# Writing a gate vector to DRAM: one transfer of single values, or a transpose and 16 rows

## Chip, core and metric

The kernel runs on one core of a Trainium2 chip. The metric is the device time of one execution in microseconds; the median over several runs is compared. The core has TensorE (PE; PEld is its weight load), VectorE (DVE), ScalarE (ACT) and GpSimd (POOL), and SyncE (SP), which here issues nearly all DMA transfers. Each engine works through its own queue in order. A DMA queue entry waits on SP until what it needs is there, and whatever stands behind it waits too.

## What is computed

A two-layer decoder trunk on x of 256 tokens by 2048. Each layer has two sub-layers, a token mixer and a SwiGLU, four sub-layers in all (0 to 3), and each is

```
mod = silu(c) @ w + b
shift, scale, gate = split(mod, 3)
x <- LayerNorm(ALPHA * x + (1 + gate) * f(x * (1 + scale) + shift))
```

c is one vector of 2048, so shift, scale and gate are vectors of 2048 per sub-layer. f is in layer 0 an mLSTM and an RWKV-7 head group between an input and an output projection, in layer 1 a retention and a gated DeltaNet group, and in both layers a SwiGLU. All is in float32.

## The kernel before

The time goes into the products with the weights. The weights come from DRAM in tiles of 128 x 2048 float32 (1 MB), by `raw` (L667), into three buffers named raw. `split` (L689 on ScalarE, L690 on VectorE) cuts each into two parts hi and lo of type float32r, and `part` (L704, L705, L706) makes three products of them. A raw buffer is free again when its second part is split, and the next load is issued on SP.

The modulation is not a TensorE product. `ada` runs 192 units, 48 for each sub-layer; a unit loads a tile of 128 x 2048 through the same three raw buffers (some of the first ones through other buffers) and multiplies it on VectorE with silu(c) and sums along the row (L634), which gives one column of 128 values. `fill` strews these units between the units of the products at a given rate, up to a limit (`ada_limit`) for each stage. So the gate of a sub-layer is long complete, in most cases, before it is used. Units 32 to 47 of a sub-layer give the gate. At unit 47, L653 forms 1 + gate in the tile g1 (128 partitions x 16 columns: value 128 k + p of the gate stands in partition p, column k).

The residual needs the gate along the free dimension, the same in all 128 partitions. For that g1 goes to a scratch tile in DRAM, gate_row, of 16 rows of 128 values (L655), and `gate_rows` fetches the 8 KB row into all 128 partitions, 1 MB in SBUF (L661). `gate_rows` is called in `mix_out` (sub-layers 0 and 2, with a buffer of the pool a) and in `ffn` ahead of the second third's down products (sub-layers 1 and 3, with a buffer of the pool y). The users of the gate are `residual` (L833) and `last_sum` (L845) on VectorE.

Small buffers go round by tag. t2 has three buffers, used for the rows of the layer norm (`ln_rows`, L819), blocks of x (`x_block`, L802), the tables of the retention heads (L1656), the weights of the mLSTM heads and others. The PSUM tag c has two banks, used for instance by the convolution's transposes (L1318). Tiles of one tag are opened in program order.

The order of the instructions on each engine is not that of the program. Class `Plan` takes all instructions with their dependences, simulates the engines with a cost for each kind of instruction, puts at each moment the ready instruction with the lowest program number next (weight loads and splits are moved up by 2000), and imposes the order that comes out. It gives a transfer the time of its bytes and a fixed part. So any new instruction can shift the order of others, and one with a low number is taken as soon as its inputs and its buffer are there.

Of the kernel before, what the change touches and what calls it, by code (L numbers as in the profile page):

```python
# [12 lines left out]
F32 = mybir.dt.float32  # L13
F32R = mybir.dt.float32r
I32 = mybir.dt.int32
AF = mybir.ActivationFunctionType
# [5 lines left out]
P = 128  # L22
T = 256
NT = T // P
D = 2048
KT = D // P
# [499 lines left out]
class Trunk:  # L526
# [97 lines left out]
    def ada_unit(self, u, deep):  # L624
        nc, v = self.nc, self.nc.vector
        sub, i = divmod(u, 48)
        src = self.ins["ada"][u]
        if deep and i % 2:
            w = self.a8([P, D])
            nc.sync.dma_start(w[:], src)  # L630
        else:
            w = self.raw(src)
        m = self.mod
        v.scalar_tensor_tensor(w[:], w[:], 1.0, self.sc[:], ALU.mult, ALU.mult, accum_out=m[:, i:i + 1])  # L634
        ob = COLS["adab"][0] + 48 * sub
        if i < 32:
            if i % 8 < 7:
                return
            g = i // 8
            s = slice(4 * g, 4 * g + 4)  # L640
            sh, sc, bi = self.tiny([P, 4])[:], self.ab[:, sub, s], self.ab[:, sub, 16 + 4 * g:20 + 4 * g]
            v.tensor_tensor(sh, m[:, i - 7:i - 3], self.cols[:, ob + i - 7:ob + i - 3], ALU.add)
            v.scalar_tensor_tensor(sc, m[:, i - 3:i + 1], 1.0, self.cols[:, ob + i - 3:ob + i + 1], ALU.add, ALU.add)
            if sub == 0:
                v.tensor_copy(bi, sh)
            else:
                og, ol = COLS["lng"][0] + 16 * (sub - 1) + 4 * g, COLS["lnb"][0] + 16 * (sub - 1) + 4 * g
                v.tensor_tensor(bi, self.cols[:, ol:ol + 4], sc, ALU.mult)
                v.tensor_tensor(bi, bi, sh, ALU.add)
                v.tensor_tensor(sc, self.cols[:, og:og + 4], sc, ALU.mult)  # L650
            return
        if i == 47:
            v.scalar_tensor_tensor(self.g1[:], m[:, 32:48], 1.0, self.cols[:, ob + 32:ob + 48], ALU.add, ALU.add)  # L653
            self.gate_row = self.dram.tile([KT, P], F32, name=self.name("gate_row"))
            nc.sync.dma_start(self.gate_row[:].rearrange("k p -> p k"), self.g1[:])  # L655

    def gate_rows(self, room, sub):

        self.ada(max(0, 48 * sub + 48 - self.ada_next))
        gate = room([P, D])  # L660
        self.nc.sync.dma_start(gate[:], self.gate_row[:].rearrange("k p -> (k p)").unsqueeze(0).to_broadcast([P, D]))  # L661
        return gate


# [1140 lines left out]
```

## Time and profile before

| | |
|---|---|
| median of 3 runs | 2866.54 us (2863.94 to 2867.68) |
| the profiled execution | 2870.13 us, span 2868.4 us |
| mean granted TensorE clock | 0.970 |
| TensorE busy | 2701.2 us, 94% |
| VectorE, ScalarE, GpSimd busy | 71%, 44%, 2% |
| DMA | 683.80 MB in 118664 packets |
| weight loads of 1 MB, issue to landing | 4.7 to 5.5 us (median by source) |

How to read it: the span is from the first to the last instruction of the profiled execution. Busy time of an engine says little about what a stage waits for; views by stretches of time give the busy time of each engine in each, the clock that TensorE was granted (1.00 is full speed) and what the DMA engines moved. The wait views name for each waiting instruction what came last. Lines such as L655 are lines of the kernel before; `SPq` marks entries of SP's DMA queue.

### The profile page before, as it was taken

Reading aid. Unit: us, or ns where it says so; the run is one execution under the profiler, and the core shown is the slowest. Engines: PE = TensorE matmul, PEld = TensorE weight load, DVE = VectorE, ACT = ScalarE, POOL = GpSimd, SP = SyncE. Lnnn points to the kernel's source line nnn. Section 1 sums busy time; section 2 is a strip of 40 time slices with the busy share of each in tenths; the row PEclk is TensorE's granted clock in tenths of the full one; section 3 lists DMA queues with packets and bytes.
Section 4 is the critical chain, followed back from the end, with each engine's and each line's share of the span. In section 5 each row is a group of like instructions: output and inputs, shape, how many; then the busy total and the mean of one; then the engine's idle time right before and its main releaser. Section 6 shows DMA issues by size and latency. Waiting matters only on the chain.

```text
span 2868.4 us, 33238 instructions
## 1 busy us (share of the span) xinstructions
PE 2701.2 (94%) x12618; PEld 2215.9 (77%) x12618; DVE 2024.6 (71%) x3189; ACT 1261.6 (44%) x1668; POOL 69.3 (2%) x88
## 2 busy tenths in 40 slices
PE   3699998899999899999999899999989999999997
PEld 2577776787778788788787788788878888888886
DVE  7789578577867547768777798876786646557557
ACT  1365344437544344343445555344454444443442
POOL 0000000100000000000000010101000000000000
PEclk9899898799999999999999999999999999999999
DMA  9878476164668768877875776575656756756554
GB/s 401 313 266 286 141 266 224 45 220 175 210 220 316 249 220 318 301 269 262 323 276 189 241 266 246 211 263 207 247 192 249 264 191 249 250 191 235 194 191 161
DMA packets 118664, 683.80 MB, mean 238 GB/s; under 512 B 20708, under 2 KB 23912, under 8 KB 40296
## 3 DMA queue, kind: packets, MB, share of 16 engines
q1 hardware_dynamic: 117064, 679.05, 65.5%
q10 hardware_dynamic: 1440, 2.62, 0.2%
q8 instruction: 99, 1.62, 0.2%
q14 instruction: 61, 0.50, 0.1%
HBM read 670.58 MB, written 11.04 MB: 238 GB/s over the span
## 4 chain that ended last, share of the span: by engine, by line
PE 60%; DMA 10%; DVE 10%; ACT 3%; issue 1%; POOL 0%; ACTq 0%; DVEq 0%; SPq 0%
PE g L705 18%; PE g L706 18%; PE g L704 18%; DMA raw<-gu 4%; DVE lo L690 3%; DVE raw L634 3%; DMA raw<-ada 2%; ACT hi L689 2%; DMA raw<-w_cd 1%; PE m L1013 1%; PE m L1020 1%; PE m L948 1%; DMA t<-lnrow 1%; DMA raw<-w_z 0%; PE m L1027 0%
## 5 line engine op out<-in xcount | busy, mean ns | idle before, releaser
L690 DVE TENSOR_TENSOR lo<-raw,hi 128x1024 fp32r<-128x1024 f32 (+3 forms) x826 | 994.3, 1212 | 612.0 <-ACT hi L689 608.6
L689 ACT ACTIVATE hi<-raw 128x1024 fp32r<-128x1024 f32 (+3 forms) x826 | 859.5, 1048 | 1232.5 <-PE g L706 854.6
L704 PE MATMUL g<-hi,h 128*128 128x512 f32 (+3 forms) x2304 | 907.5, 395 | 81.2 <-ACT hi L689 53.6
L705 PE MATMUL g<-lo,h 128*128 128x512 f32 (+3 forms) x2304 | 908.9, 395 | 18.0 <-DVE lo L690 17.6
L706 PE MATMUL g<-hi,h 128*128 128x512 f32 (+3 forms) x2304 | 903.2, 393 | 0.0
L704 PEld LDWEIGHTS g<-hi,h 128*128 128x128 f32 x2304 | 440.0, 191 | 176.3 <-ACT hi L689 58.9
L705 PEld LDWEIGHTS g<-lo,h 128*128 128x128 f32 x2304 | 440.3, 191 | 118.8 <-DVE lo L690 32.9
L706 PEld LDWEIGHTS g<-hi,h 128*128 128x128 f32 x2304 | 439.9, 191 | 85.1 <-issue 1.3
L634 DVE SCALAR_TENSOR_TENSOR raw<-raw,silu_c 128x2048 f32<-128x2048 f32 x176 | 402.8, 2289 | 49.3 <-DMA raw<-ada 48.1
L704 PE MATMUL g<-hi,a 128*128 128x512 f32 x920 | 360.3, 392 | 6.8 <-DVE t L845 5.4
L705 PE MATMUL g<-lo,a 128*128 128x512 f32 x920 | 360.5, 392 | 0.8 <-DVE lo L690 0.8
L706 PE MATMUL g<-hi,a 128*128 128x512 f32 x920 | 359.8, 391 | 0.0
L704 PEld LDWEIGHTS g<-hi,a 128*128 128x128 f32 x920 | 173.2, 188 | 43.8 <-DVE t L845 6.1
L705 PEld LDWEIGHTS g<-lo,a 128*128 128x128 f32 x920 | 173.4, 188 | 37.8 <-DVE lo L690 2.4
L706 PEld LDWEIGHTS g<-hi,a 128*128 128x128 f32 x920 | 173.3, 188 | 35.8 <-DVE a L748 0.5
L1324 DVE SCALAR_TENSOR_TENSOR f<-c,cols_sb,f 128x253 f32<-128x253 f32 (+2 forms) x120 | 56.5, 477 | 5.7 <-ACT f L1321 4.9
L1519 POOL TENSOR_SCALAR s<-cons_sb,log_alpha 128x128 f32<-128x128 f32 x16 | 19.0, 1202 | 1058.9 <-DVE log_alpha L1463 895.8
L634 DVE SCALAR_TENSOR_TENSOR a<-a,silu_c 128x2048 f32<-128x2048 f32 x16 | 36.2, 2286 | 1.3 <-DMA a<-ada 1.2
L887 ACT ACTIVATE t<-m,affine 128x128 f32<-128x128 f32 x96 | 34.9, 467 | 0.1
L1028 ACT ACTIVATE y<-m 128x512 f32<-128x512 f32 x24 | 14.0, 597 | 44.2 <-PE m L1027 43.1
L1184 PE MATMUL m<-y 64*128 64x256 f32 x128 | 31.1, 454 | 2.2 <-DVE a L1187 1.9
L951 ACT ACTIVATE a<-m 128x512 fp32r<-128x512 f32 x44 | 26.0, 591 | 14.8 <-PE m L948 13.5
(426 smaller groups left out, 2138.4 us busy)
## 6 DMA issues: line engine op xcount, KB each, us to landing
raw<-ada SPq DMA_DIRECT2D x176, 1024.0 KB, 5.4
raw<-gu SPq DMA_DIRECT2D x176, 1024.0 KB, 5.5
raw<-dn SPq DMA_DIRECT2D x88, 1024.0 KB, 4.8
raw<-w_cd SPq DMA_DIRECT2D x60, 1024.0 KB, 4.9
raw<-w_ab SPq DMA_DIRECT2D x56, 1024.0 KB, 5.3
a<-ada SPq DMA_DIRECT2D x16, 1024.0 KB, 15.3
raw<-o_ab SPq DMA_DIRECT2D x16, 1024.0 KB, 4.7
raw<-o_cd SPq DMA_DIRECT2D x16, 1024.0 KB, 4.8
```

The source lines that it names most:

```text
L634: v.scalar_tensor_tensor(w[:], w[:], 1.0, self.sc[:], ALU.mult, ALU.mult, accum_out=m[:, i:i + 1])
L689: nc.scalar.activation(hi[:, :2 * n], ws, AF.Copy)
L690: nc.vector.tensor_tensor(lo[:, :2 * n], ws, hi[:, :2 * n], ALU.subtract)
L704: mm(o, ah, wh, start=start and k == 0, stop=False)
L705: mm(o, ah, wl, start=False, stop=False)
L706: mm(o, al, wh, start=False, stop=stop and k == 3)
L887: nc.scalar.activation(h32[:, j, :], b[:, P * j:P * j + P], AF.Identity, bias=self.ab[:, sub + 1, 16 + k:17 + k], scale=self.ab[:, sub + 1 ...
L948: nc.tensor.transpose(b[:, P * k:P * k + P], gs[:, t, P * k:P * k + P], self.ident)
L1013: nc.tensor.matmul(x[:, 64 * j:64 * j + 64], mt[:, hs.start + j, :], dv[:, hs.start + j, :, 0, :], start=True, stop=True)
L1020: nc.tensor.matmul(x[:, 256 + 64 * j:320 + 64 * j], dt[:, hs.start + j, :], y[:, j, :], start=True, stop=True)
L1184: mm(b[:, T * x:T * x + T], bk[r, c, x, t, :], ar[r, c, t].rearrange("p x s -> p (x s)"), start=True, stop=True)
L1324: v.scalar_tensor_tensor(o[:, d:T], b[:, T * j:T * j + T - d], self.col(wname, 4 * (tile0 + i + j) + 3 - d), o[:, d:T], ALU.mult, ALU.add)
```

## The change

The write at ada unit 47 is taken out. `gate_rows` now first transposes g1 on TensorE (with the identity matrix, into 16 partitions x 128 columns of a PSUM bank of tag c), copies that on ScalarE to a t2 tile, writes its 16 partitions to DRAM as 16 rows of 512 bytes, and then fetches the gate as before. The write before took the values in the order of g1, so neighbouring values of a partition went to DRAM 512 bytes apart. The DRAM tile is now local to the call.

```diff
         if i == 47:
             v.scalar_tensor_tensor(self.g1[:], m[:, 32:48], 1.0, self.cols[:, ob + 32:ob + 48], ALU.add, ALU.add)
-            self.gate_row = self.dram.tile([KT, P], F32, name=self.name("gate_row"))
-            nc.sync.dma_start(self.gate_row[:].rearrange("k p -> p k"), self.g1[:])
 
     def gate_rows(self, room, sub):
 
         self.ada(max(0, 48 * sub + 48 - self.ada_next))
+        b = self.bank("c")
+        self.nc.tensor.transpose(b[:KT, 0:P], self.g1[:], self.ident)
+        short = self.t2([P, P])
+        self.nc.scalar.activation(short[:KT, :], b[:KT, 0:P], AF.Copy)
+        row = self.dram.tile([KT, P], F32, name=self.name("gate_row"))
+        self.nc.sync.dma_start(row[:], short[:KT, :])
         gate = room([P, D])
-        self.nc.sync.dma_start(gate[:], self.gate_row[:].rearrange("k p -> (k p)").unsqueeze(0).to_broadcast([P, D]))
+        self.nc.sync.dma_start(gate[:], row[:].rearrange("k p -> (k p)").unsqueeze(0).to_broadcast([P, D]))
         return gate
```

## The prediction

> **What bounds the kernel now.** I read the page's busy shares first, then the answer for the tile gate_row, then busy time by stretches behind each of its four writes, then the waits there.
>
> ```profile
> span 2868.4 us, 33238 instructions
> PE 2701.2 (94%) x12618; PEld 2215.9 (77%) x12618; DVE 2024.6 (71%) x3189; ACT 1261.6 (44%) x1668; POOL 69.3 (2%) x88
> ...
> DMA packets 118664, 683.80 MB, mean 238 GB/s; under 512 B 20708, under 2 KB 23912, under 8 KB 40296
> ```
>
> TensorE is busy 94% of the span, so a microsecond is won where TensorE idles or runs at a lower clock, about 167 us of idle time in all. Everything else counts only through that.
>
> ```profile
> L655 SPq DMA_DIRECT2D gate_row<-one_and_gate x4: 377/380/387, 279.2 to 2468.6; - x4
> L661 SPq DMA_DIRECT2D a<-gate_row x2: 327/562/797, 638.8 to 2034.7; - x2
> L661 SPq DMA_DIRECT2D y<-gate_row x2: 326/374/423, 1005.7 to 2481.6; - x2
> ```
>
> The write of L655 runs four times, once per sub-layer; the timeline of SP's queue has the starts:
>
> ```profile
> 279.18 0.38 SPq L655 DMA_DIRECT2D gate_row<-one_and_gate  x1
> ...
> 954.18 0.39 SPq L655 DMA_DIRECT2D gate_row<-one_and_gate  x1
> ...
> 1623.59 0.38 SPq L655 DMA_DIRECT2D gate_row<-one_and_gate  x1
> ```
>
> The fourth is the 2468.6 above. Now the stretches behind each (busy us and count of PE, PEld, DVE, ACT, POOL; granted clock; DMA share; GB/s):
>
> ```profile
> 283.00:294.00 11.00, 10.65 (x87) 9.91 (x85) 9.06 (x23) 6.42 (x11) 0.00 (x0) 1.00 0.75 45
> 294.00:303.00 9.00, 3.19 (x22) 2.58 (x21) 2.79 (x5) 1.26 (x3) 0.00 (x0) 0.88 0.81 329
> 303.00:322.00 19.00, 18.92 (x82) 18.02 (x82) 4.45 (x7) 4.73 (x10) 0.10 (x1) 0.52 0.38 125
> 322.00:326.00 4.00, 4.00 (x29) 3.30 (x27) 0.85 (x2) 0.53 (x2) 0.00 (x0) 1.00 0.01 2
> 958.00:969.00 11.00, 9.28 (x40) 7.03 (x38) 4.51 (x4) 1.06 (x1) 0.00 (x0) 1.00 0.71 34
> 969.00:974.00 5.00, 0.18 (x1) 0.18 (x1) 0.20 (x1) 1.29 (x2) 0.00 (x0) 0.58 0.89 347
> 974.00:980.00 6.00, 5.53 (x13) 3.96 (x14) 5.59 (x5) 1.77 (x2) 0.00 (x0) 0.50 0.86 344
> ...
> 1626.00:1638.00 12.00, 10.63 (x45) 7.92 (x43) 6.00 (x8) 3.38 (x5) 0.00 (x0) 1.00 0.58 33
> 1638.00:1644.00 6.00, 0.24 (x1) 0.25 (x2) 3.19 (x4) 2.35 (x5) 0.00 (x0) 0.85 0.75 305
> 1644.00:1656.00 12.00, 12.00 (x59) 12.00 (x59) 5.93 (x10) 4.00 (x9) 0.00 (x0) 0.51 0.62 212
> 1656.00:1660.00 4.00, 4.00 (x36) 4.00 (x35) 3.66 (x8) 1.67 (x4) 0.00 (x0) 1.00 0.39 150
> 2462.00:2472.00 10.00, 10.00 (x46) 8.28 (x45) 6.30 (x7) 4.21 (x4) 0.00 (x0) 1.00 0.77 279
> 2472.00:2482.00 10.00, 10.00 (x50) 8.23 (x49) 6.85 (x8) 4.30 (x6) 0.00 (x0) 1.00 0.42 40
> ```
>
> See the last column. Some 4 us behind each write, when what was queued before it has drained, the transfers fall to 33 to 45 GB/s for 10 to 12 us, four times out of four, where 279 GB/s ran just before. The DMA engines are not idle meanwhile (share 0.42 to 0.75): they are moving single values. Behind the first three, TensorE then runs dry and comes back at half clock for 6 to 19 us; behind the fourth it does not. The waits in those places name the late party:
>
> ```profile
> DVE raw L634 <- DMA raw<-ada: 7.0, 2, 6.2
> ...
> ACT hi L689 <- DMA raw<-gu: 13.7, 2, 12.8
> ...
> ACT hi L689 <- DMA raw<-w_z: 7.1, 1, 7.1
> ```
>
> (waiter, releaser, us in total, times, longest). Weight tiles issued behind the write arrive late: in the first place an ada tile that holds VectorE, and with it the work queued behind; in the other two tiles that ScalarE has to split before TensorE can start.
>
> **Part by part. (1) The strided write goes.** Idle of TensorE, length minus busy in the rows above: first 0.35 + 5.81 + 0.08 = 6.2; second 1.72 + 4.82 + 0.47 = 7.0; third 1.37 + 5.76 = 7.1; fourth 0. Together 20.4 us. Half clock: the first stretch of 18.92 busy us at 0.52 would take 9.8 at full clock, so 9.1 are lost; by counts, 82 matmuls at the 29 in 4 us of the stretch behind take 11.3, so 7.6. Second: 5.53 at 0.50, 2.8. Third: 12.00 at 0.51, 5.9; by counts 59 at 36 in 4 us, 6.6, so 5.4. Together 15.8 to 17.8. The stalls cost 36 to 38 us; I take 37. In the three places VectorE and ScalarE stand still too (0.20 and 1.29 of 5 us in 969 to 974), so no other engine is getting ahead meanwhile.
>
> The Trainium skill (TensorE: Matmul & The Clock Gate, Part 1) says that a busy window of about 3.4 us restores the full clock. By that rule the half clock would be worth 1.7 us a place, 5 in all, and the stalls 25.5; the rows with 18.9 and 12.0 busy us at half clock do not bear it out, so the rows decide.
>
> **(2) What the stall gave back.** While TensorE stood, the weight buffers filled:
>
> ```profile
> 240.00:279.00 39.00, 36.58 (x172) 28.88 (x171) 35.05 (x73) 14.55 (x19) 0.00 (x0) 1.00 0.86 314
> 326.00:372.00 46.00, 45.70 (x202) 34.06 (x202) 37.30 (x113) 23.78 (x46) 3.68 (x5) 1.00 0.53 188
> ```
>
> Before the first write TensorE idled 2.4 us in 39, after it 0.3 in 46. If those 46 us had idled like the earlier ones, 2.8 us, then 2.5 come back as small waits. The same in all three places would make 7.5; in none, 0. I take 4, about the middle.
>
> **(3) What is added**, four times: a transpose, a ScalarE copy, a small write, and a fetch that waits for it.
>
> ```profile
> L1637 PE MATMUL c<-cons_sb,zt x32: 270/272/273, 1828.0 to 1975.3; 128*128 128x128 f32 x32
> ...
> L1186 ACT ACTIVATE a<-m x32: 265/269/305, 195.4 to 547.4; 128x128 f32<-128x128 f32 x32
> ...
> x<-y SPq DMA_DIRECT2D x24, 256.0 KB, 2.4
> ...
> SPq L667 <- DVE lo L690: 1322.9, 333, 13.0
> ...
> SPq L661 <- DMA gate_row<-one_and_gate: 7.9, 1, 7.9
> ```
>
> The transpose is at most a 0.27 us matmul: 4 x 0.27 = 1.1 us on TensorE, paid in full. The copy, 0.27 us, four times, sits in ScalarE's 56% of free time: nothing; without that cover 1.1. The write of 16 rows: stores of 256 KB land in 2.4 us, so 2.4 is the upper end and 0.4 (its issue) the lower; SP's queue, in order, stands that long before the fetch, with weight loads queued behind it. SP waits 1322.9 us for buffers to come free anyhow, and the 7.9 us wait before the fourth fetch passed with TensorE fully busy (row 2472 to 2482): nothing. Without that cover, 2.4 a place, 9.6.
>
> **(4) What moves.** The write leaves SP's queue behind ada unit 47 and stands directly ahead of the fetch, in gate_rows; its order against the loads is the planner's, which sees 8 KB as nearly free in either form. The copy's tile takes one of three t2 buffers, the transpose one of two c banks. Who needs the gate, and when:
>
> ```profile
> L833 DVE TENSOR_TENSOR y<-y,a x16: 681/684/687, 685.3 to 2066.1; 128x512 f32<-128x512 f32 x16
> L833 DVE TENSOR_TENSOR y<-y,y x16: 677/681/685, 1279.8 to 2656.5; 128x512 f32<-128x512 f32 x16
> ...
> L1318 PE MATMUL c<-cons_sb,zt x16: 270/272/328, 661.8 to 678.6; 128*128 128x128 f32 x16
> ...
> 2014.65 0.33 SPq L1656 DMA_DIRECT2D t<-ret  x1
> 2017.38 3.04 SPq L819 DMA_DIRECT2D t<-lnrow  x2
> ...
> PE g L704 <- DVE t L845: 5.4, 1, 5.4
> ...
> y<-gate_row SPq DMA_DIRECT2D x2, 1024.0 KB, 6.9
> ```
>
> Sub-layers 1 and 3 use y tiles; sub-layer 1 has from its write at 954 until 1279.8. In sub-layer 0 the c banks go to the convolution (L1318) until 678.6; transpose, copy, write and fetch then need about 0.3 + 0.3 + 2.4 + 6.9 = 10 us and end near 689, where L833 wants the gate at 685.3: 4 us late at worst, on VectorE. In sub-layer 2 the copy needs the t2 buffer that went to lnrow at 2017.4 and holds it some 3 us; the fetch stood at 2034.7, later than that, so it need not move. If it did, the residual chain there, which already ends in a 5.4 us wait of TensorE, would lengthen by as much, 3 us. Between 0 and 7; I take 2, nearer 0 because both have other work between.
>
> **Sum.** -37 + 4 + 1.1 + 2 = -30 us. The profiled execution took 2870.1, 3.6 above the median of the three runs, 2866.5; against that median, 2837. With every term at its good end (-38, 0, 1.1, 0) it is 2829.5, at its bad end (-36, 7.5, 2.2, 7) 2847; the three runs themselves spread over 3.7, so 2826 to 2848.
>
> **The rivals.** A: only part of it shows. All engines are reordered by the planner once the new instructions are in, and a new stall like that wait of 5.4 us, with a clock drop as behind the second write (2.8), costs 8 to 10 us. One to three of those, or more given back: 2848 to 2861. B: nothing changes, because the write was not what starved the loads; the ada stream is added traffic in the same places. Against it: four starvations behind four writes, and the 7.9 us that the fetch waited for one of them. It would give 2861 to 2872. The Trainium skill (DMA: Bandwidth & Descriptors, Anatomy of one DMA) fits a transfer as 2.0 us plus bytes, by which 8 KB costs 2 us in either form and B would hold; the 10 to 12 us measured here speak against it. C, on the other side: SP's queue. The write stands behind a ScalarE copy and the fetch behind the write, and weight loads stand behind both; where the three weight buffers happen to be empty, TensorE runs dry as it did behind the first write, 6.2 + 9 = 15 us a place. Two places eat the gain; from the third on (45 against 30) the kernel is slower: 2881, with four 2896. For it: the page shows such a wait lead to half clock three times. Against it: the wait is 2.4 us where those starvations lasted 10.
>
> **How the numbers follow.** Forecast 66%, 2826 to 2848; A 18%; B 7%; C 9%. The time is the forecast's, 2837. The range 2825 to 2861 leaves out B and C, 16%. A change of 0.2%, 5.7 us, is about what a measurement here can tell from none: faster 0.84 (forecast and A), same 0.07, slower 0.09.
>
> **What would show it.**
>
> ```profile
> core 0: 2868.4 us, clock 0.970
> ```
>
> Packets should fall by 4 x 2048 - 4 x 16 to about 110,540, those under 512 B to about 12,500. No stretch of 10 us near 285, 960 and 1628 at under 50 GB/s; no half clock at 303 to 322, 974 to 980 and 1644 to 1656; mean clock from 0.970 to about 0.978 (the stretches above lack 9 + 1 + 2 + 3 + 1 + 6 = 22 us of full clock, 0.8% of the span). The fetch's wait for gate_row should be under 3 us each. Wrong would be: the starvation still there (B), SP waits at the new write or the fetch with TensorE idle behind them (C), or new idle elsewhere of 8 us and more (A).

## Result, and the profile after

| | before | changed |
|---|---|---|
| median of 4 runs | 2865.24 us (2856.41 to 2867.68) | 2831.11 us (2826.44 to 2837.96) |
| profiled execution | 2870.13 us | 2830.83 us |

The ratio is 0.9888, 95% interval 0.9859 to 0.9918: faster by 1.1%, where 1.0% was forecast (2837 against 2866.5). Measured once more, beside the kernels below, it was 0.9872, 0.9850 to 0.9895.

The page of the changed kernel, the same rows as were shown of before, and the mean clock, 0.977 where about 0.978 was forecast:

```profile
span 2829.1 us, 33250 instructions
PE 2684.7 (95%) x12622; PEld 2204.3 (78%) x12622; DVE 2023.7 (72%) x3189; ACT 1260.0 (45%) x1670; POOL 72.0 (3%) x88
...
DMA packets 110536, 683.80 MB, mean 242 GB/s; under 512 B 12516, under 2 KB 15784, under 8 KB 32168
...
core 0: 2829.1 us, clock 0.977
```

The packets fell by 8128, which is 4 x 2048 less 4 x 16, and those under 512 B by 8192. This agrees with the Trainium skill (DMA: Bandwidth & Descriptors, Rules for kernel authors): a last dimension that is not contiguous goes out as one descriptor per element.

Where ada unit 47 now ends (L653), nothing is written any more. The rows of that line in the changed kernel: all four, and the second and the third alone.

```profile
L653 DVE SCALAR_TENSOR_TENSOR one_and_gate<-modulation,cols_sb x4: 165/170/177, 276.5 to 2429.0; 128x16 f32<-128x16 f32 x4
...
L653 DVE SCALAR_TENSOR_TENSOR one_and_gate<-modulation,cols_sb x1: 177/177/177, 928.9 to 928.9; 128x16 f32<-128x16 f32 x1
L653 DVE SCALAR_TENSOR_TENSOR one_and_gate<-modulation,cols_sb x1: 165/165/165, 1588.5 to 1588.5; 128x16 f32<-128x16 f32 x1
```

The stretches behind these points in the changed kernel (busy us and count of PE, PEld, DVE, ACT, POOL; clock; DMA share; GB/s):

```profile
283.00:294.00 11.00, 11.00 (x90) 10.44 (x89) 10.26 (x26) 4.94 (x10) 0.00 (x0) 1.00 0.52 193
294.00:303.00 9.00, 9.00 (x72) 8.28 (x71) 4.04 (x5) 4.60 (x10) 0.00 (x0) 1.00 0.64 201
303.00:322.00 19.00, 18.70 (x96) 13.06 (x96) 9.74 (x39) 7.86 (x26) 3.47 (x5) 1.00 0.22 80
934.00:945.00 11.00, 11.00 (x50) 9.02 (x49) 9.06 (x7) 3.34 (x4) 0.00 (x0) 1.00 0.74 285
945.00:956.00 11.00, 9.54 (x45) 7.20 (x44) 7.17 (x10) 5.21 (x6) 0.00 (x0) 1.00 0.77 282
1589.00:1601.00 12.00, 12.00 (x54) 9.94 (x53) 9.47 (x14) 7.42 (x13) 0.00 (x0) 1.00 0.72 256
1601.00:1607.00 6.00, 5.21 (x40) 5.00 (x39) 4.96 (x7) 3.10 (x7) 0.00 (x0) 0.87 0.43 141
1607.00:1619.00 12.00, 10.05 (x63) 9.69 (x63) 10.70 (x26) 5.58 (x10) 3.26 (x2) 0.78 0.56 199
```

The stretches at 33 to 45 GB/s are gone; 193, 285 and 256 GB/s stand in their place. So is the idle TensorE behind the first write, with its half clock. Some of the gain is given back: 1.46 us idle in 945 to 956, 2.74 in 1601 to 1619, and in this last stretch the clock is 0.78 to 0.87.

### The profile page after: what moved, and what is told of

The parts are those of the page before. It is cut to its first block, busy times and chain, and to the rows that moved or that the text cites. A ratio compares the mean times of both kernels' runs of the same rounds, so it can differ in the third digit from the quotient of the medians.

```text
span 2829.1 us, 33250 instructions
## 1 busy us (share of the span) xinstructions
PE 2684.7 (95%) x12622; PEld 2204.3 (78%) x12622; DVE 2023.7 (72%) x3189; ACT 1260.0 (45%) x1670; POOL 72.0 (3%) x88
## 4 chain that ended last, share of the span: by engine, by line
PE 64%; DVE 9%; DMA 8%; ACT 2%; issue 1%; POOL 0%; DVEq 0%; ACTq 0%
PE g L709 19%; PE g L710 19%; PE g L708 19%; DMA raw<-gu 3%; DVE lo L694 3%; DMA raw<-ada 2%; DVE raw L634 2%; ACT hi L693 1%; PE m L1017 1%; PE m L1024 1%; DMA t<-x 1%; DMA raw<-w_cd 1%; PE m L952 1%; DMA raw<-dn 1%; PE m L1031 0%
## 5 line engine op out<-in xcount | busy, mean ns | idle before, releaser
L709 PE MATMUL g<-lo,h 128*128 128x512 f32 (+3 forms) x2304 | 905.4, 393 | 12.1 <-DVE lo L694 11.9
L634 DVE SCALAR_TENSOR_TENSOR a<-a,silu_c 128x2048 f32<-128x2048 f32 x16 | 36.2, 2288 | 1.3 <-DMA a<-ada 1.0
L955 ACT ACTIVATE a<-m 128x512 fp32r<-128x512 f32 x44 | 25.9, 591 | 13.6 <-PE m L952 12.5
```

What stands on the lines that cost most here:

```text
L709: mm(o, ah, wl, start=False, stop=False)
```

## Experiments

The planner re-plans every engine once an instruction is added, so the changed kernel differs from before in more than the write. The theories: T, the single values occupy the DMA engines, weight tiles behind them come late, and TensorE runs dry and then at half clock; O, the new order is what gained; P, taking the write away from unit 47 is what gained. A kernel that keeps the old order word for word tells them apart.

**Runs of 64 bytes.** The gate's columns of the modulation weights and bias are arranged in DRAM so that partition p of g1 holds values 16p to 16p+15 (in the cut below, `a` is a copy of the weights or of the bias). The write then goes out as 128 runs of 64 bytes. On TensorE, VectorE, ScalarE and GpSimd the instructions and their order are those of before, and on SP only the form of these four writes differs.

```diff
-            self.gate_row = self.dram.tile([KT, P], F32, ...)
-            nc.sync.dma_start(self.gate_row[:].rearrange("k p -> p k"), self.g1[:])
+            self.gate_row = self.dram.tile([KT // 16, P, 16], F32, ...)
+            nc.sync.dma_start(self.gate_row[:].rearrange("a p b -> p a b"), self.g1[:].rearrange("p (a b) -> p a b", b=16))
...
+    g = a[..., 2 * D:]
+    a[..., 2 * D:] = np.moveaxis(g.reshape(g.shape[:-1] + (KT // 16, P, 16)), -1, -2).reshape(g.shape)
```

> The kernel before with the order of all engines' instructions unchanged; only the four writes of L655 differ: the columns of the gate's weights and bias are laid out in DRAM so that partition p of g1 holds the neighbouring values 16p to 16p+15, and a write is 128 runs of 64 bytes. No transpose, no copy, no move. Theory T (single values occupy the DMA engines): the three stalls go, minus 33 to minus 39 us, 2827 to 2833, and no stretch of 10 us under 50 GB/s behind the writes. Rival O (the gain of the changed kernel comes from the new order of instructions): 2860 to 2870, as before. Rival P (the gain comes from taking the write away from ada unit 47): 2860 to 2870.

Measured: 2831.24 us (2821.23 to 2836.57) against 2858.64 of before beside it; ratio 0.9908 (0.9886 to 0.9929). Its page and stretches, the first place and the third:

```profile
DMA packets 110984, 683.80 MB, mean 242 GB/s; under 512 B 13028, under 2 KB 16232, under 8 KB 32616
...
283.00:294.00 11.00, 11.00 (x90) 10.43 (x90) 9.84 (x24) 4.57 (x10) 0.00 (x0) 1.00 0.64 207
294.00:303.00 9.00, 9.00 (x73) 8.30 (x72) 3.86 (x4) 4.23 (x9) 0.00 (x0) 1.00 0.62 217
...
1592.00:1604.00 12.00, 12.00 (x54) 9.95 (x53) 11.87 (x18) 8.32 (x15) 0.00 (x0) 1.00 0.77 285
1604.00:1610.00 6.00, 6.00 (x45) 5.78 (x44) 4.03 (x8) 3.78 (x9) 0.00 (x0) 0.86 0.70 253
1610.00:1622.00 12.00, 12.00 (x82) 11.99 (x83) 9.23 (x17) 4.81 (x10) 0.55 (x1) 0.79 0.58 204
```

The gain is there with the old order and without any move. O and P fall as its main cause. The medians differ by 27 us, less than the expected 33 to 39. Those were worked out from one profiled execution, and the two profiled executions differ by 40 (2870.13 and 2830.12); measured once more, further down, the medians differ by 36.

**Runs of 16 and of 8 bytes**, the same edit with b=4 and b=2: 512 and 1024 pieces in a write.

> As the kernel with runs of 64 bytes, but runs of 16 bytes, 512 in each write, a quarter of the 2048 pieces of before; same order of instructions. T: the starved stretch shrinks to about a quarter, 2.5 to 3 us, which the three weight buffers cover: 2827 to 2836. O and P: 2860 to 2870. If the time of a transfer does not go with its pieces but with its layout as such, 2860 to 2870 too.

> Order of before, runs of 8 bytes: 1024 pieces in a write, half of before. T, if the time goes with the pieces: the starved stretch is 5 to 6 us, about one weight tile of TensorE's work, and mostly covered by the three buffers: 2832 to 2848, between the kernel before and the runs of 16 bytes. If it goes with bytes or with the layout as such: as before.

Measured: 16 bytes 2834.41, ratio 0.9921 (0.9899 to 0.9943); 8 bytes 2832.47, ratio 0.9898 (0.9875 to 0.9920). Neither can be told from the runs of 64 bytes. Of the runs of 8 bytes, whose first write starts at 274.1, the stretches behind it:

```profile
276.00:278.00 2.00, 2.00 (x16) 1.75 (x15) 1.83 (x5) 1.75 (x2) 0.00 (x0) 1.00 1.02 287
278.00:280.00 2.00, 2.00 (x11) 1.36 (x10) 1.59 (x2) 0.63 (x2) 0.00 (x0) 1.00 1.28 209
280.00:282.00 2.00, 2.00 (x16) 1.77 (x14) 1.02 (x2) 2.00 (x3) 0.00 (x0) 1.00 0.76 131
282.00:284.00 2.00, 2.00 (x19) 1.92 (x18) 1.13 (x4) 1.51 (x4) 0.00 (x0) 1.00 0.95 336
```

Half the pieces leave a dip of about 4 us, to 209 and then 131 GB/s, and TensorE stays busy, where all 2048 made 11 us at 45 GB/s. So the loss does not grow evenly with the pieces: the short dip costs nothing that can be measured. That loaded weight buffers bridge it is the likely reason; how full they were was not measured. For 8 bytes I had expected up to 12 us above the runs of 16, which did not come.

**The old write put back into the changed kernel**, to a scratch tile that nobody reads.

```diff
+            nc.sync.dma_start(self.dram.tile([KT, P], F32, ...)[:].rearrange("k p -> p k"), self.g1[:])
```

> The changed kernel with the old strided write of g1 put back at ada unit 47, to a scratch tile that nobody reads. T: the stalls come back, 2855 to 2872. O: the new order stays nearly as it is, so 2826 to 2838. P: 2855 to 2872, as under T.

Measured: 2860.93 us, ratio 1.0000 (0.9983 to 1.0017) to the kernel before. The whole gain is gone again. Its DMA issues (size, median us from issue to landing), and the stretches behind its first spare write at 275.0:

```profile
spare<-one_and_gate SPq DMA_DIRECT2D x4, 8.0 KB, 13.1
...
279.00:290.00 11.00, 9.89 (x80) 9.02 (x78) 8.38 (x21) 6.32 (x10) 0.00 (x0) 1.00 0.80 64
290.00:299.00 9.00, 4.33 (x31) 3.72 (x30) 3.84 (x7) 1.26 (x3) 0.00 (x0) 0.94 0.74 303
299.00:318.00 19.00, 19.00 (x90) 17.76 (x88) 3.87 (x5) 4.74 (x10) 0.10 (x1) 0.58 0.36 125
```

The picture of before returns, although the traces show the four compute engines in the order of the changed kernel, and SP too but for the four writes put in. No one waits for these writes: they harm only by what is queued behind them. This is the strongest evidence for T. Whether the loads are held up in the queue or at the DMA engines, no run here tells apart.

The write lands after 13.1 us; as 128 runs of 64 bytes, also at unit 47, it lands after 4.4. The fit of 2.0 us plus bytes, cited for rival B from the Trainium skill (DMA: Bandwidth & Descriptors, Anatomy of one DMA), stands there for transfers issued from GpSimd. These are issued on SP, and the fit, which has no term for the pieces, does not describe them.

**The place without the layout.** The changed kernel in its own order, its writes in gate_rows as 2048 single values.

```diff
-        row = self.dram.tile([KT, P], F32, name=self.name("gate_row"))
-        self.nc.sync.dma_start(row[:], short[:KT, :])
+        row = self.dram.tile([P, KT], F32, name=self.name("gate_row"))
+        self.nc.sync.dma_start(row[:].rearrange("p k -> k p"), short[:KT, :])
...
```

> The changed kernel with the order of all engines unchanged, but its four writes in gate_rows go out as 2048 single values (the layout of the gate's weights makes the result the same). T: 10 us of starvation behind each write, and the fetch waits 10 us or more for it; at most one or two of the four places have empty weight buffers, so 0 to 25 us slower than the changed kernel: 2831 to 2856, with the stretches under 50 GB/s visible. O: 2826 to 2838. P: 2826 to 2838, because the place alone counts.

Measured: 2855.75 us, ratio 0.9984 (0.9967 to 1.0002). The move alone gains next to nothing, the upper end of what T allowed. The fetch's waits on SP; the stretches behind the first write (668.5) and behind the second fetch (1242.6); and three rows of the timeline in the first place (start, us, what, and in brackets the idle time before it and what ended it):

```profile
SPq L665 <- DMA gate_row<-t: 29.4, 3, 11.2
...
668.00:680.00 12.00, 12.00 (x58) 9.51 (x56) 5.77 (x15) 9.54 (x14) 0.41 (x1) 1.00 0.49 61
680.00:690.00 10.00, 3.46 (x12) 2.87 (x12) 4.63 (x6) 0.74 (x2) 0.00 (x0) 0.69 0.57 208
1243.00:1250.00 7.00, 3.50 (x16) 2.56 (x14) 0.74 (x2) 1.06 (x1) 0.00 (x0) 1.00 0.88 288
...
684.86 0.69 DVE L837 TENSOR_TENSOR y<-y,a 128x512 f32<-128x512 f32 x1 [10.56 <-DMA a<-gate_row]
685.47 1.22 DVE L694 TENSOR_TENSOR lo<-raw,hi 128x1024 fp32r<-128x1024 f32 x1
...
686.74 0.79 PE L709 MATMUL g<-lo,a 128*128 128x512 f32 x1 [6.54 <-DVE lo L694]
```

In these two places the loss comes about in another way than in the kernel before. In the first the write is late, so the fetch is late (SP waits 7.4 us for it), and VectorE stands 10.56 us at L837 for the gate. VectorE's part of the split of a weight tile that has arrived (ScalarE split its part from 676.1 on) stands behind that, and TensorE runs dry for 6.54 us and comes back at a lower clock. In the second SP stands 11.2 us at the fetch, the next loads are issued only behind it, from 1242.9 on, and TensorE idles 3.50 of 7 us: that is rival C's mechanism. With rows of 512 bytes the waits are too short for either. So this run says little about starved loads: the 61 GB/s of the first row are also due to SP, which issued a single load between the write and the fetch. And since the move brought waits of its own, P falls by the runs of 64 bytes rather than by this run.

**The layout without the move**: transpose, copy and the write of 16 rows at unit 47.

```diff
         if i == 47:
...
+            b = self.bank("c")
+            nc.tensor.transpose(b[:KT, 0:P], self.g1[:], self.ident)
+            short = self.t2([P, P])
+            nc.scalar.activation(short[:KT, :], b[:KT, 0:P], AF.Copy)
...
-            nc.sync.dma_start(self.gate_row[:].rearrange("k p -> p k"), self.g1[:])
+            nc.sync.dma_start(self.gate_row[:], short[:KT, :])
```

> The layout alone, without the move: transpose, copy and the write of 16 rows stand at ada unit 47, where the strided write stood, and the fetch waits in gate_rows as before. A third order of instructions. T: as fast as the changed kernel, 0.8 to 1.3% under before. P: as before, within 0.2%.

Measured: 2831.11 us, ratio 0.9898 (0.9874 to 0.9922). P fell already; a third order of instructions gives the same gain. The write did not quite stay in its place, though: the planner put the first one at 325.7, where it was at 279.2 in the kernel before.

**The changed kernel and the runs of 64 bytes side by side**, unedited.

> The changed kernel once more, beside the kernel with runs of 64 bytes on the same chip. T: both lack the single values, so both are 0.8 to 1.3% faster than before; the transposes and the later fetch cost the changed kernel 0 to 3 us against the runs of 64 bytes. O: if the new order were worth something of its own, the changed kernel would be 5 us or more faster than the runs of 64 bytes, which keep the old order.

> The runs of 64 bytes once more (order of before, no transpose). T: 0.8 to 1.3% faster than before and 0 to 3 us faster than the changed kernel. O: 5 us or more slower than the changed kernel.

Measured: 2826.08 and 2825.92 us, ratios 0.9872 (0.9850 to 0.9895) and 0.9888 (0.9861 to 0.9916). No difference can be told: neither a worth of the new order nor a cost of the transposes shows. The six runs of 64 bytes spread from 2821.42 to 2843.43 us, so a difference of 5 us, O's threshold, is not strictly excluded. The runs of 64 bytes do the same with no added instruction, so they are the simpler version, not a faster one.

**One place at a time.** Order of before; one sub-layer's write as single values, the other three as runs of 64 bytes.

```diff
+            r = 1 if sub == S else KT; self.gate_row = self.dram.tile([KT // r, P, r], F32, ...)
+            nc.sync.dma_start(self.gate_row[:].rearrange("a p b -> p a b"), self.g1[:].rearrange("p (a b) -> p a b", b=r))
...
```

> Order of before; the write of sub-layer 0 goes out as single values as before, the other three as runs of 64 bytes. T, by the prediction's stretches: the first place alone costs 6.2 us idle and 7.6 to 9.1 us of half clock, about 15 of the 37: 12 to 17 us above the runs of 64 bytes, 2838 to 2848. If the first stall were given back later: 0 to 5 above.

> As before, single values in sub-layer 1 alone. T: 7.0 idle and 2.8 half clock, about 10 us: 7 to 11 above the runs of 64 bytes, 2833 to 2842.

> As before, single values in sub-layer 2 alone. T: 7.1 idle and 5.4 to 5.9 half clock, about 13 us: 10 to 14 above the runs of 64 bytes, 2836 to 2845.

> As before, single values in sub-layer 3 alone. T: starved 10 us like the others, but TensorE had three full buffers and did not idle: 0 to 2 above the runs of 64 bytes, 2826 to 2833. If each starvation cost by itself, whatever the buffers: 10 or more above.

| single values in | median us (range) | ratio to before, 95% | above the fourth alone |
|---|---|---|---|
| sub-layer 0 | 2843.62 (2836.46 to 2850.99) | 0.9910 (0.9877 to 0.9944) | 13.5 |
| sub-layer 1 | 2845.88 (2837.13 to 2848.24) | 0.9920 (0.9897 to 0.9944) | 15.8 |
| sub-layer 2 | 2842.23 (2840.03 to 2843.70) | 0.9913 (0.9894 to 0.9932) | 12.1 |
| sub-layer 3 | 2830.11 (2822.47 to 2830.67) | 0.9865 (0.9843 to 0.9887) | 0 |
| all four (before) | 2866.29 (2860.16 to 2871.71) | 1 | 36.2 |

Three places cost 12 to 16 us each, 41.4 together, against 36.2 with all four: additive within the scatter. The second came out above its expected 7 to 11, but its range reaches down to 7.0 above. The fourth, to which the last column compares the others, costs nothing that can be measured: its ratio of 0.9865 lies beside the 0.9908 and 0.9888 of the kernel with runs of 64 bytes in all four. Yet it starves like the others; the kernel with single values in sub-layer 3 alone, behind its write at 2420.8:

```profile
2420.00:2424.00 4.00, 4.00 (x20) 3.30 (x19) 2.05 (x3) 1.83 (x2) 0.00 (x0) 1.00 1.00 363
2424.00:2434.00 10.00, 10.00 (x50) 8.24 (x49) 4.04 (x5) 2.83 (x5) 0.00 (x0) 1.00 0.72 52
```

At 52 GB/s for 10 us TensorE stays busy for 10.00 of 10.00. What differs there is the queue: in the kernel before, ada tiles, which give TensorE no work, are issued among the weight tiles behind the first three writes (286.5, 963.5 and 1628.4), but none behind the fourth, whose ada unit is the last. So more of the three buffers hold work for TensorE there. That this is why the fourth is free fits the rows, but no run changed it alone.

## Why the prediction was right, step by step

**The stalls (37).** Shown. Because the runs of 64 bytes keep the order of before, points of the two profiled executions can be compared one to one. The lead of the later kernel, by first or last issues of the same loads:

| point | before | runs of 64 bytes | lead |
|---|---|---|---|
| write of sub-layer 0 | 279.2 | 275.9 | 3.3 |
| first gu load (behind the first place) | 763.3 | 743.0 | 20.3 |
| first w_cd load (behind the second) | 1526.2 | 1495.3 | 30.9 |
| last w_z load (behind the third) | 1656.8 | 1614.8 | 42.0 |
| last y_out store | 2865.1 | 2825.0 | 40.1 |

So the places give 17.0, 10.6, 11.1 and, with all that follows, -1.9; the prediction had 14 to 15, 9.8, 12.5 to 13 and 0. The sum of the first three is 38.7 against 37. In the same stretches TensorE's idle time fell by 10.7, 5.6 and 7.0 us, where 6.2, 7.0 and 7.1 were forecast, and its busy time, which the half clock lengthens, by 6.3, 5.0 and 4.1, where 7.6 to 9.1, 2.8 and 5.4 to 5.9 were forecast. So both parts are real, but single parts were off by up to 4.5 us and partly offset each other; that the sum came so close is in part luck. The lead of 3.3 ahead of the first write is not due to the change.

One reading on the way was too wide: VectorE and ScalarE stood still in 969 to 974, but not in all three places. VectorE was busy 2.79 of 9 us in 294 to 303 and 3.19 of 6 in 1638 to 1644.

**Given back (4).** Not found. The small waits of TensorE that were to come back did not: behind the third place too its idle time is lower in the runs of 64 bytes (26.7 us) than in the kernel before (28.9). In the changed kernel the idle time of the whole span fell from 167.2 to 144.4 us, by 22.8, more than the 20.4 forecast for the stalls alone. What does take back some gain is the clock: in the runs of 64 bytes it falls to 0.86 and 0.79 in 1604 to 1622 (rows above), 0.8 + 2.5 = 3.4 us lost, where the half clock of the third place had cost 5.9. But the leads of the table are net of that: 40.1 less 3.3 is 36.8, so by this pair of executions almost nothing of the 37 was given back. The term was too large, and its reason was wrong: I had put it down to empty weight buffers, and what shows is the clock.

**Added (1.1, and 0 for the copies and waits).** The transpose and the waits in the changed kernel; the rows from 1219.05 to 1227.54 are from the timeline of SP's queue (start, us, what), the last is the stretch there:

```profile
L659 PE MATMUL c<-cons_sb,one_and_gate x4: 271/272/272, 671.2 to 2525.8; 128*16 128x128 f32 x4
...
SPq L665 <- DMA gate_row<-t: 12.3, 3, 6.4
...
1219.05 0.33 SPq L671 DMA_DIRECT2D raw<-dn  x1
1219.42 0.90 SPq L823 DMA_DIRECT2D t<-lnrow  x2
1220.65 0.45 SPq L663 DMA_DIRECT2D gate_row<-t  x1
1227.54 0.33 SPq L665 DMA_DIRECT2D y<-gate_row  x1
...
1220.00:1228.00 8.00, 8.00 (x41) 6.69 (x40) 4.87 (x6) 3.83 (x6) 0.00 (x0) 1.00 0.61 212
```

4 x 0.27 us held. The write of 16 rows was mis-sized: it landed after 3.8 us (median of the four), where 2.4 was taken as the upper end. The longest wait of the fetch was predicted under 3 us and came to 6.4; there, one load of 1 MB and two of 256 KB were issued in the 1.6 us ahead of the write, which is the likely reason. It cost nothing: TensorE was busy 8.00 of 8.00 us. That it would be covered was the step that mattered.

**Moved (2).** In sub-layer 0 VectorE was to wait 4 us at worst for the gate, and waited 3.7:

```profile
DVE y L837 <- DMA a<-gate_row: 3.7, 1, 3.7
...
671.00:684.00 13.00, 13.00 (x64) 10.55 (x63) 8.79 (x19) 10.54 (x16) 1.17 (x1) 1.00 0.45 165
...
PE g L708 <- DVE t L849: 5.3, 1, 5.3
```

TensorE was busy through it, so the term was 0. In sub-layer 2 the wait of TensorE at the end of the residual chain is 5.3 us, 5.4 before: the chain did not lengthen.

**Against which time.** The profiled executions differ by 39.3 us (2870.13 and 2830.83), the medians by 34.1, and by 35.6 when measured once more, where the sum said 30. The two terms that did not show, 4 given back and 2 for the move, are about the size of this miss: -37 + 1.1 alone is -36. Executions of the kernel before ran from 2848.6 to 2869.1 in one set, so a sum made on one of them carries about 10 us either way.

**The rivals.** B is excluded by the result and by the old write put back. C's mechanism showed with single values in gate_rows, but not with rows of 512 bytes. A's new stalls did not come: the idle time fell by more than was forecast.

## What to carry to other kernels

Look at the pieces of a DMA, not only at its bytes: behind 8 KB sent as 2048 single values the core's transfers ran at 33 to 64 GB/s for 10 to 12 us, while 1024 pieces and fewer cost nothing that could be measured. So a transfer that nobody waits for can be the cause of a stall elsewhere. Look for it in the GB/s of the stretches behind its issue. The cheapest cure may be to lay the producer's data out so that each partition holds neighbouring values, which needs no transpose at all. And such a stretch need not cost anything: three places lost 12 to 16 us each, the fourth none, so ask what work for the bounding engine is already loaded.

## Not expected

- The step between 1024 pieces of 8 bytes (a dip of about 4 us, no loss) and 2048 of 4 bytes (10 to 12 us) is more than the count explains. The landings say the same: medians of 4.4, 6.1 and 7.7 us for writes of 128, 512 and 1024 pieces, but 13.1 for the spare write of 2048. They include what was queued ahead of the write. Whether a piece of 4 bytes takes longer than one of 8 was not measured apart.
- The clock was at 0.79 in 1610 to 1622 of the runs of 64 bytes, with TensorE busy 12.00 of 12.00 us and 6.00 of 6.00 before it. So a lower clock does not need an idle stretch right ahead of it; what set it off here stays open.
